# A list scheduler's stated durations and engine-to-engine times, both set to those of the trace: a two-block fp32 model on one core

## The chip, the cores and the metric

The kernel runs on one core of a Trainium2 chip. The metric is the device time of one execution in microseconds (us), taken as the median over runs. The core's engines are TensorE (PE, with its weight loads listed apart as PEld), VectorE (DVE), ScalarE (ACT), GpSimd (POOL) and SyncE (SP), which issues the large DMAs here. Each engine works through its own list of instructions in the order in which they were emitted; semaphores hold an instruction until what it reads is there.

## What is computed

Two blocks on 512 tokens of width 1024, all in fp32. Cut to its frame:

```python
def first_block(x, mem, ...):
    for i in range(2):
        h = _rms_norm(x, norm_mix_pre[i]); mem_n = _rms_norm(mem, mem_norm[i])
        if i == 0:
            mixed = _attention_sublayer(h, mem_n, ...)   # 12 heads of 64 in 3 dilated bands, relative bias
        else:
            mixed = _deltanet_sublayer(h, mem_n, ...)    # 6 heads of 128, both directions, chunked
        x = x + _rms_norm(mixed, norm_mix_post[i])
        h = _rms_norm(x, norm_ffn_pre[i])
        x = x + _rms_norm(_swiglu(h, ffn_w_gate_up[i], ffn_w_down[i]), norm_ffn_post[i])
    return x

def second_block(x, ...):
    h = rmsnorm(x, norm_g); proj = h @ w_in
    mix = concat([gla_mixer(...), s5_mixer(...), nsa_mixer(...)])
    return x + mix @ w_out
```

Both sublayers of the first block also attend to a memory of 256 rows and end in an output projection. In the DeltaNet sublayer a recurrent state runs over the chunks of a head:

```python
def step(state, inp):                       # one chunk
    v_new = uc - wc @ state
    out = (qc * exp(gc)) @ state + ac @ v_new
    state = state * exp(g_last) + (kc * exp(g_last - gc)).T @ v_new
```

## The kernel before

Activations live on chip as 128-partition tiles, transposed for the matmuls (`X`: 8 k-tiles of 128x512). Every large matmul is `mm3` (L265 to L273): each operand is a pair of high and low part in fp32r, and a product is three passes, L271 (high by low), L272 (low by high), L273 (high by high). The passes of 128x512 in such a triple are called rows below, three of them a triple. Weights come by SP's DMA into three `raw` buffers; ACT writes the high part (L243, `wh`), and DVE, or POOL for the pieces marked `aside`, the low part (L262, `wl`), each as two halves of 128x512; four pairs exist (`wsl`).

The layers follow one another in `layers` (from L1728): the attention front, `out_ffn` 0, the DeltaNet layer, `out_ffn` 1, the second block. `out_ffn` takes an output projection through `X` and the swiglu FFN behind it. `projector` (L1788 on) supplies projections that fill PE between the steps of the heads, with a large `late` (a low rank); the output projection of the layer belongs to the thread `trunk` and ranks lower still.

**What sets the order.** No order is written out by hand. Every piece of the program is a generator, a thread of the class `Flow` (L48 to L147). Before it emits an instruction it yields an engine, a stated cost, and the tokens that it waits for. A token holds a stated time and the engine that made it. `start` gives the earliest stated start: the time at which the engine is free, and for each token its time plus a stated way from engine to engine. `run` takes the operation with the earliest start, and among those of the same engine that could start within 0.1 of it the one with the lowest `late`. It books start plus cost as the end, on the engine and as the token of the thread, and lets the thread emit. So the stated numbers decide which instruction stands before which in each engine's list, and the chip then runs the lists as they are. The stated costs come from small formulas:

```python
def act(n, ap=0): return "ACT", 0.1 + n * 8.4e-4 + 0.1 * ap
def dve(n):       return "DVE", 0.07 + n * 1.05e-3
def pool(n):      return "POOL", 0.1 + n * 2.4e-3
```

and from numbers at the yields: 0.65 for a triple of 128x512 (0.33 for one of 256 columns), 0.22 for a single small matmul.

**Names that come up later.** At the start, x and the memory are normalized and transposed: `norm` makes the sum of squares on ACT, adds eps on DVE (L338, `iss`), raises to -1/2 on POOL (L340, `irs`), scales on DVE (L343, L346, `hs`), and PE transposes (L354, `hT`). The other norms do the same (L917 to L956; `hs` at L942, transpose L949, `Xh` and `Xl` L951, L956). In the front, L769 weights the heads' outputs and L796 makes the `Xl` that the output projection reads. In the DeltaNet layer `each` prepares a head: convolutions on DVE (four L1324 and one L1305 for each of key, query and value), decays (L1405, L1413, L1422) and the inverse of a unit triangular matrix by blocks (PE L1503, L1519, L1523, L1544, L1566; ACT L1530; DVE L1506, L1548, L1571). `chain` (L1594 to L1633) then walks four chunks for each direction d: PE L1594, DVE `rhs` L1597, PE L1602, ACT `vn` L1605, DVE `vs` L1610, PE L1612, DVE `St` L1616 or L1619, outputs at PE L1624 and L1625, summed at DVE L1629 (`otok`). `gate_out` (L1640 to L1661) normalizes a head's output (ACT L1651, POOL L1352 and L1658), transposes it (PE L1335, `poT`) and gates it; L1706 and L1708 split it into the `Xh`, `Xl` of the output projection. At the end of the second block, softmax units (L2720 to L2753) alternate with triples of the last output projection.

## Time and profile before

| | |
|---|---|
| median of 3 runs | 1763.38 us (1762.12 to 1763.65) |
| the profiled execution | 1761.48 us, span 1759.5 us, mean granted clock 0.993 |
| PE busy | 1708.7 us (97%) in 12031 matmuls |
| DVE, ACT, POOL busy | 979.8 us (56%), 763.2 us (43%), 338.0 us (19%) |
| chain that ended last | PE 84%, DVE 9%, ACT 2%, issue 2% |

A row of the timeline gives the start, the duration, engine and line, the operation and its tiles; xN stands for N alike in a row, with the time from the first start to the last end; the bracket is the engine's idle time before it and what ended that. A row of the waits gives for whom PE waited, the sum, the number of times and the longest. Windows give the busy time of each engine in a stretch, and PEclk, the share of the full clock that TensorE was granted.

### The profile page before, as it was taken

To read this page: it belongs to the slowest core of one execution; us is meant where nothing else is said; L and a number is where in the kernel's file an instruction comes from. 1 tells how busy PE (TensorE), PEld (TensorE's weight loads), DVE (VectorE), ACT (ScalarE), POOL (GpSimd) and SP (SyncE) were. 2 spreads that over 40 slices of the span, in tenths; PEclk is the share of its full clock that TensorE was granted. 3 is DMA by queue.
4 is the path that set the end of the run, shared out by engine and by line. 5 is a ranking of instruction groups with operands and counts; after the bars stand their busy time and mean duration, and the time that the engine had idled before them with its cause. 6 is when DMAs were issued, how large, how long until landed. Compare 5 with 4: busy or idle time off the path is not lost.

```text
span 1759.5 us, 30190 instructions
## 1 busy us (share of the span) xinstructions
PE 1708.7 (97%) x12031; PEld 1423.2 (81%) x12031; DVE 979.8 (56%) x1997; ACT 763.2 (43%) x1808; POOL 338.0 (19%) x496
## 2 busy tenths in 40 slices
PE   6999999999999999999999899999999999999999
PEld 5988679888888888788777788888888888888787
DVE  6333656323333378867887467464433468467573
ACT  5443635333223245656555355333223353345671
POOL 5200001000000021220222351364540033210000
PEclk9999999999999999999999999999999999999999
DMA  6513133333233332211110164345333253552012
GB/s 195 154 51 95 49 120 97 120 96 96 96 96 96 96 114 79 61 38 38 38 37 32 59 152 139 109 133 144 108 108 96 77 159 115 153 154 69 25 37 84
DMA packets 211981, 167.84 MB, mean 95 GB/s; under 512 B 21996, under 2 KB 183036, under 8 KB 211840
## 3 DMA queue, kind: packets, MB, share of 16 engines
q1 hardware_dynamic: 203808, 154.39, 29.7%
q0 software_dynamic: 4560, 9.42, 2.1%
q10 hardware_dynamic: 3472, 2.10, 0.4%
q8 instruction: 94, 1.54, 0.4%
q14 instruction: 47, 0.39, 0.1%
HBM read 152.23 MB, written 13.65 MB: 94 GB/s over the span
## 4 chain that ended last, share of the span: by engine, by line
PE 84%; DVE 9%; ACT 2%; issue 2%; DMA 1%; POOL 1%; ACTq 0%; SPq 0%; DVEq 0%; POOLq 0%
PE bk L271 23%; PE bk L272 22%; PE bk L273 22%; DVE hn L1324 2%; DVE wl L262 1%; PE no L2753 1%; PE npT L2736 1%; PE x L1519 1%; PE x L1523 1%; PE y L1544 1%; DVE hs L942 1%; PE ns L2722 1%; PE hT L949 1%; PE ns L2720 1%; PE o L1625 1%
## 5 line engine op out<-in xcount | busy, mean ns | idle before, releaser
L262 DVE TENSOR_TENSOR wl<-raw,wh 128x512 fp32r<-128x512 f32 x450 | 315.8, 742 | 372.4 <-ACT wh L243 371.8
L243 ACT ACTIVATE wh<-raw 128x512 fp32r<-128x512 f32 x474 | 273.0, 623 | 534.4 <-PE bk L273 300.4
L271 PE MATMUL bk<-Xh,wl 128*128 128x512 f32 (+2 forms) x1312 | 494.9, 377 | 0.2 <-ACT Xh L951 0.2
L272 PE MATMUL bk<-Xl,wh 128*128 128x512 f32 (+2 forms) x1312 | 478.4, 365 | 0.5 <-DVE Xl L956 0.5
L273 PE MATMUL bk<-Xh,wh 128*128 128x512 f32 (+2 forms) x1312 | 478.5, 365 | 0.0
L273 PEld LDWEIGHTS bk<-Xh,wh 128*128 128x128 f32 (+1 forms) x1312 | 246.9, 188 | 40.1
L271 PEld LDWEIGHTS bk<-Xh,wl 128*128 128x128 f32 (+1 forms) x1312 | 247.5, 189 | 39.0 <-issue 3.5
L272 PEld LDWEIGHTS bk<-Xl,wh 128*128 128x128 f32 (+1 forms) x1312 | 247.7, 189 | 34.8 <-DVE Xl L956 0.9
L271 PE MATMUL bk<-wh,Xl 128*128 128x512 f32 (+1 forms) x424 | 152.6, 360 | 6.7 <-DVE Xl L796 3.7
L272 PE MATMUL bk<-wl,Xh 128*128 128x512 f32 (+1 forms) x424 | 145.8, 344 | 0.3 <-DVE wl L262 0.2
L273 PE MATMUL bk<-wh,Xh 128*128 128x512 f32 (+1 forms) x424 | 145.2, 342 | 0.0
L271 PE MATMUL bk<-wh,Al 128*128 128x512 f32 x352 | 139.7, 397 | 0.0
L272 PE MATMUL bk<-wl,Ah 128*128 128x512 f32 x352 | 139.5, 396 | 0.0
L921 POOL TENSOR_TENSOR nc<-ncm,nhalf 128x1 f32<-128x1 f32 x16 | 11.5, 720 | 661.9 <-DVE ncm L919 661.9
L273 PE MATMUL bk<-wh,Ah 128*128 128x512 f32 x352 | 138.6, 394 | 0.0
L1093 DVE TENSOR_TENSOR sg<-sg,bk 128x512 f32<-128x512 f32 x44 | 30.2, 687 | 124.7 <-PE bk L273 120.2
L271 PEld LDWEIGHTS bk<-wh,Xl 128*128 128x128 f32 x424 | 84.7, 200 | 18.0 <-DVE Xl L796 3.1
L273 PEld LDWEIGHTS bk<-wh,Xh 128*128 128x128 f32 x424 | 84.8, 200 | 8.1
L272 PEld LDWEIGHTS bk<-wl,Xh 128*128 128x128 f32 x424 | 85.0, 200 | 7.6 <-DVE wl L262 1.0
L271 PEld LDWEIGHTS bk<-wh,Al 128*128 128x128 f32 x352 | 66.0, 188 | 16.1
L273 PEld LDWEIGHTS bk<-wh,Ah 128*128 128x128 f32 x352 | 66.0, 188 | 16.0
L272 PEld LDWEIGHTS bk<-wl,Ah 128*128 128x128 f32 x352 | 66.1, 188 | 15.4
(586 smaller groups left out, 2623.8 us busy)
## 6 DMA issues: line engine op xcount, KB each, us to landing
raw<-in_ffn_w_gate_up_dram SPq DMA_DIRECT2D x88, 512.0 KB, 3.9
raw<-in_ffn_w_down_dram SPq DMA_DIRECT2D x44, 512.0 KB, 3.3
raw<-in_dn_w_in_dram SPq DMA_DIRECT2D x27, 512.0 KB, 4.0
raw<-in_att_w_in_dram SPq DMA_DIRECT2D x20, 512.0 KB, 4.1
raw<-in_w_in_dram SPq DMA_DIRECT2D x20, 512.0 KB, 3.8
raw<-in_mem_w_kv_dram SPq DMA_DIRECT2D x8, 512.0 KB, 3.6
raw<-in_att_w_out_dram SPq DMA_DIRECT2D x8, 512.0 KB, 3.3
xd<-x SPq DMA_DIRECT2D x8, 512.0 KB, 2.6
```

The source lines that it names most:

```text
L243: nc.scalar.activation(wh[:, sl], ev["raw"][:, sl], AF.Copy)
L262: eng.tensor_tensor(wl[:, sl], raw[:, sl], wh[:, sl].bitcast(F32), op=OP.subtract)
L271: mm(out, A[1], B[0], start=first, stop=False, **kw)
L272: mm(out, A[0], B[1], start=False, stop=False, **kw)
L273: mm(out, A[0], B[0], start=False, stop=last, **kw)
L942: nc.vector.scalar_tensor_tensor(hh[:, hv[i]], x[:, t, hv[i]], r2, r["gain"][:, hv[i]], op0=OP.mult, op1=OP.mult)
L949: nc.tensor.transpose(p[:, k * P:(k + 1) * P], hh[:, i * 512 + k * P:i * 512 + (k + 1) * P], self.ident)
L1093: nc.vector.tensor_tensor(sg, sg, pu, op=OP.mult)
L1324: nc.vector.scalar_tensor_tensor(acc[:, d0:d1], raw[:, d0 + o:d1 + o], cw[:, ti, tap:tap + 1], acc[:, d0:d1], op0=OP.mult, op1=OP.add)
L1519: nc.tensor.matmul(dn8(b[i])[at], lhsT, rhs, start=True, stop=True)
L1523: nc.tensor.transpose(b[d][:, o:o + P], U[:, d, 2 * n:2 * n + 2, :].rearrange("p c q -> p (c q)"), self.ident)
L1544: nc.tensor.matmul(dn8(ys[par])[HB[f], d, n, :], T[d][HB[par], n, f, :], xs[f][HB[par], d, n, :], start=True, stop=True)
```

## The change

The ways from engine to engine are stated by pair: 0.2 from PE, 0.12 to PE, 0.04 between ACT, DVE and POOL (before: 0.2 for all), and nothing on the same engine (before: 0.07). Every DVE operation is booked 0.08 longer and every ACT operation 0.07 longer, on the engine too. A triple is booked at 0.682 and 0.36 in place of 0.65 and 0.33. Costs of POOL and of the DMA stay. No instruction is added, removed or changed; the engines' lists hold the same instructions in another order. With three lines more, L271 is L274 after the change, and so on.

```diff
-    HOP = 0.2
+    HOP = 0.04
+    FROM_PE, TO_PE = 0.2, 0.12
+    STEP = {"DVE": 0.08, "ACT": 0.07}
...
-            s = max(s, at + (self.HOP if e != eng else 0.0 if e == "PE" else 0.07))
+            s = max(s, at + (self.FROM_PE if e == "PE" else self.TO_PE if eng == "PE" else self.HOP) * (e != eng))
...
             eng, cost = t["req"][:2]
+            cost += self.STEP.get(eng, 0.0)
             self.free[eng] = s + cost
...
-                t = yield "PE", 0.65 * (t1 - t0) / S
+                t = yield "PE", 0.682 * (t1 - t0) / S
...
-                        t = yield "PE", 0.33
+                        t = yield "PE", 0.36
```

In the FFN stretches the lists stay as they were. Elsewhere matmul triples and steps of the heads change places. Three places follow.

POOL at the start: the powers (`irs`) of the token norms and the low parts of the first weights. Before:

```order
L340 TENSOR_TENSOR irs<-iss,nhalf 128x1
L262 TENSOR_TENSOR wl<-raw,wh 128x512 x3
L340 TENSOR_TENSOR irs<-iss,nhalf 128x1
L262 TENSOR_TENSOR wl<-raw,wh 128x512 x2
L340 TENSOR_TENSOR irs<-iss,nhalf 128x1
L262 TENSOR_TENSOR wl<-raw,wh 128x512 x2
```

After:

```order
L343 TENSOR_TENSOR irs<-iss,nhalf 128x1 x2
L265 TENSOR_TENSOR wl<-raw,wh 128x512 x3
L343 TENSOR_TENSOR irs<-iss,nhalf 128x1 x2
L265 TENSOR_TENSOR wl<-raw,wh 128x512 x2
L462 DMA bias_scr<-brow 4x3x384
```

The second of these powers stood behind three low parts and stands ahead of them now; PE's transposes of the token norms follow two by two.

DVE in the third head of the DeltaNet layer, where `chain` and the convolutions of a later head share it. Before:

```order
L1597 SCALAR_TENSOR_TENSOR rhs0_7948<-chain_7776,neg_5158,vtok_6811 128x128
L1324 SCALAR_TENSOR_TENSOR hn_7904<-craw_7902,convw_881,hn_7904 128x511
L1610 TENSOR_SCALAR vs1_7964<-vn1_7956,ksc_5156 128x128
L1324 SCALAR_TENSOR_TENSOR hn_7904<-craw_7902,convw_881,hn_7904 128x511
L1610 TENSOR_SCALAR vs0_7991<-vn0_7966,ksc_5156 128x128
L1616 SCALAR_TENSOR_TENSOR St1_7993<-St1_7884,etot_5157,chain_7820 128x128
```

After:

```order
L1600 SCALAR_TENSOR_TENSOR rhs0_7922<-chain_7745,neg_5160,vtok_6936 128x128
L1509 COPY_PREDICATED U_7746<-lm64_892,y0_7906 64x256 x2
L1308 SCALAR_TENSOR_TENSOR vTh_7609<-sqt_7904,hn_7630 128x512
L1613 TENSOR_SCALAR vs0_7961<-vn0_7935,ksc_5158 128x128
L1613 TENSOR_SCALAR vs1_7964<-vn1_7959,ksc_5158 128x128
L1327 SCALAR_TENSOR_TENSOR hn_7915<-craw_7913,convw_894,hn_7915 128x510
L1619 SCALAR_TENSOR_TENSOR St0_7976<-St0_7894,etot_5159,chain_7745 128x128
L1619 SCALAR_TENSOR_TENSOR St1_7979<-St1_7864,etot_5159,chain_7823 128x128
L1327 SCALAR_TENSOR_TENSOR hn_7915<-craw_7913,convw_894,hn_7915 128x511 x2
```

Both `vs` stood behind a convolution step each; now they stand together, behind other work of the inverse, and ahead of the convolution.

PE in the last head of the DeltaNet layer, where the chain of the head and the triples of the output projection (`wh`, `Xl`) meet. Before:

```order
L1612 MATMUL chain<-vs_9742,ktok 128x128
L1594 MATMUL chain<-St_9740,kTh 128x128
L1624 MATMUL o<-St_9710,qe_9081 128x128
L1625 MATMUL o<-vn_9735,AT_9055 128x128
L271 MATMUL bk<-wh,Xl 128x512
L272 MATMUL bk<-wl,Xh 128x512
L273 MATMUL bk<-wh,Xh 128x512
L1602 MATMUL chain<-rhs_9755,Uf 128x128
L1594 MATMUL chain<-St_9750,kTh 128x128
```

After:

```order
L1615 MATMUL chain<-vs_9764,ktok 128x128
L1627 MATMUL o<-St_9737,qe_9038 128x128
L1628 MATMUL o<-vn_9757,AT_9024 128x128
L1627 MATMUL o<-St_9742,qe_9172 128x128
L1628 MATMUL o<-vn_9761,AT_9133 128x128
L1597 MATMUL chain<-St_9767,kTh 128x128
L1597 MATMUL chain<-St_9772,kTh 128x128
L1605 MATMUL chain<-rhs_9781,Uf 128x128
L1605 MATMUL chain<-rhs_9783,Uf 128x128
```

The triples are gone from between the chain's steps: all 22 that stood from the head's L1544 to its `poT` now stand ahead of that L1544.

## Rows read from the trace of the kernel before

**Rows 1.** PE's waits: waiter, line, releaser; us in total, times, longest, whole span.

```profile
PE chain L1612 <- DVE vs L1610: 5.3, 5, 1.4
PE hT L949 <- DVE hs L942: 4.7, 9, 1.4
PE bk L271 <- DVE Xl L796: 3.7, 2, 2.8
...
PE hT L354 <- DVE hs L346: 2.8, 2, 2.3
```

**Rows 2.** Windows: startup, an FFN, the DeltaNet layer's two halves, the last softmax units.

```profile
core 0: us, PE busy (x) PEld busy (x) DVE busy (x) ACT busy (x) POOL busy (x), PEclk, DMA share, GB/s
0.00:48.00 48.00, 33.46 (x198) 29.00 (x199) 30.42 (x44) 27.91 (x52) 28.64 (x36) 0.93 0.67 198
...
290.00:630.00 340.00, 340.00 (x1536) 280.87 (x1536) 120.13 (x191) 103.37 (x188) 0.54 (x1) 1.00 0.33 99
...
684.00:860.00 176.00, 173.53 (x2004) 141.15 (x2004) 138.20 (x315) 107.15 (x293) 38.52 (x31) 0.99 0.17 46
860.00:979.00 119.00, 110.97 (x1521) 91.75 (x1519) 91.63 (x202) 63.21 (x175) 29.49 (x25) 0.97 0.12 37
```

**Rows 3.** Windows: two of the stretches at a lower clock, and the last softmax units.

```profile
31.60:38.40 6.80, 6.80 (x28) 5.36 (x27) 2.98 (x4) 1.94 (x5) 6.09 (x7) 0.50 0.56 190
...
943.00:946.40 3.40, 3.05 (x13) 2.84 (x14) 3.37 (x7) 0.28 (x1) 1.44 (x2) 0.50 0.00 0
...
1700.00:1718.00 18.00, 18.00 (x142) 14.30 (x142) 9.51 (x29) 11.37 (x46) 0.00 (x0) 1.00 0.01 1
```

**Rows 4.** Timeline of DVE at the start (start, us): two in a row, one.

```profile
12.03 1.28 DVE L367 TENSOR_TENSOR hn<-hT,gm 128x512 f32<-128x512 f32 x2
13.23 0.68 DVE L262 TENSOR_TENSOR wl<-raw,wh 128x512 fp32r<-128x512 f32 x1
```

**Rows 5.** Timeline of POOL at the start.

```profile
21.23 0.94 POOL L340 TENSOR_TENSOR irs<-iss,nhalf 128x1 f32<-128x1 f32 x1 [9.74 <-DVE iss L338]
22.16 5.24 POOL L262 TENSOR_TENSOR wl<-raw,wh 128x512 fp32r<-128x512 f32 x3
```

**Rows 6.** Timeline of all engines, third head of the DeltaNet layer.

```profile
859.20 1.44 DVE L1324 SCALAR_TENSOR_TENSOR hn<-craw,convw,hn 128x511 f32<-128x511 f32 x1
...
860.57 1.28 DVE L1610 TENSOR_SCALAR vs<-vn,ksc 128x128 f32<-128x128 f32 x1
...
861.90 0.38 PE L1612 MATMUL chain<-vs,ktok 128*128 128x128 f32 x1 [1.37 <-DVE vs L1610]
```

**Rows 7.** Timeline of PE, an earlier head: the chain's three links, with other work between.

```profile
747.49 0.61 PE L1594 MATMUL chain<-St,kTh 128*128 128x128 f32 x4
748.64 0.61 PE L1602 MATMUL chain<-rhs,Uf 128*128 128x128 f32 x4
749.78 0.42 PE L1612 MATMUL chain<-vs,ktok 128*128 128x128 f32 x2
...
751.70 0.39 PE L1612 MATMUL chain<-vs,ktok 128*128 128x128 f32 x2
752.62 0.38 PE L1594 MATMUL chain<-St,kTh 128*128 128x128 f32 x2
```

**Rows 8.** Timeline of PE, the last head of the DeltaNet layer.

```profile
976.61 0.33 PE L1544 MATMUL y<-xT 64*64 64x64 f32 x4 [0.94 <-ACT xT L1530]
...
978.43 0.47 PE L271 MATMUL bk<-wh,Xl 128*128 128x512 f32 x1 [0.66 <-DVE Xl L1708]
...
983.56 0.60 PE L1602 MATMUL chain<-vtok,Uf 128*128 128x128 f32 x4
...
997.50 0.39 PE L1602 MATMUL chain<-rhs,Uf 128*128 128x128 f32 x2
...
1006.28 0.50 PE L271 MATMUL bk<-wh,Xl 128*128 128x512 f32 x1 [2.23 <-DVE Xl L1708]
```

More of the change, by code (lines that the diff above doesn't have):

```diff
@@ L412, in memory @@
                         w, kk = W["mv"][l][k // 4]["W"], k % 4
-                        t = yield "PE", 0.33
+                        t = yield "PE", 0.36
                         self.mm3(p[:, :256], (M[l].h[:, k, ts], M[l].l[:, k, ts]), (w.h[:, kk, :], w.l[:, kk, :]),
@@ L623, in group @@
                     w, kk = W2[k // 4]["W"], k % 4
-                    t = yield "PE", 0.33
+                    t = yield "PE", 0.36
                     self.mm3(p[:, :256], (X.h[:, k, t0:t0 + P], X.l[:, k, t0:t0 + P]), (w.h[:, kk, :], w.l[:, kk, :]),
@@ L1118, in out_ffn @@
                             for k in range(KT):
-                                tk = yield "PE", 0.65 * (t1 - t0) / 512
+                                tk = yield "PE", 0.682 * (t1 - t0) / 512
                                 self.mm3(p[:, t0:t1], (ev["W"].h[:, k, :], ev["W"].l[:, k, :]),
@@ L1801, in part @@
             for k in range(KT):
-                t = yield "PE", 0.65 * (t1 - t0) / S
+                t = yield "PE", 0.682 * (t1 - t0) / S
                 self.mm3(it["p"][:m, t0:t1], (W.h[:, k, :], W.l[:, k, :]), (X.h[:, k, t0:t1], X.l[:, k, t0:t1]),
@@ L1839, in projector @@
                     W, kk = it[k // 4]["W"], k % 4
-                    t = yield "PE", 0.33
+                    t = yield "PE", 0.36
                     self.mm3(p[:, :256], (X.h[:, k, sl], X.l[:, k, sl]), (W.h[:, kk, :], W.l[:, kk, :]),
@@ L2398, in glu @@
                     for k in range(2):
-                        t = yield "PE", 0.65
+                        t = yield "PE", 0.682
                         self.mm3(p, (w.h[:, k, os_], w.l[:, k, os_]), yh[k], k == 0, k == 1)
```

## The prediction

> **What bounds the kernel now.** I read the page first: PE is busy for 97% of the span, so a new order can win no more than PE's idle time and its slow-clock time, while it can lose as much as it uncovers. The windows say where the idle time lies. An FFN stretch has none (340 us busy of 340), and the lists are unchanged there, so I cost it at nothing. The startup has 48 - 33.46 = 14.5 us, of which the first wait for data is outside the change. The DeltaNet layer has 2.5 us in its first half and 119 - 110.97 = 8.0 us in the second [rows 2]. The list of waits then says on what: the chain's L1612 behind DVE's `vs` (5.3 us), the norm transposes L949 (4.7), the output projection behind L796 (3.7), the start's transposes L354 behind the wider scalings (2.8) [rows 1]. Last, the windows at a lower clock: for 6.8 us at the start and in pieces of 3.4 us later, the granted clock is 0.50, half of 2.4 GHz, each time just behind a cluster of such waits [rows 3]. A piece of 3.4 us at half rate does 1.7 us of work, so it loses 1.7 us.
>
> **What the change does to each term.** No instruction is added, so PE's work is the same sum; I only count idle time. The sum is made against the profiled execution, 1761.48 us; the median of the runs is 1.9 us above it, and I add that at the end.
>
> First, are the new numbers truer? In a pair, two DVE operations of 128x512 take 1.28 us together, but one alone 0.68 [rows 4]: a second one begins 0.60 after the first. The old formula gives 0.07 + 512 x 0.00105 = 0.608 for one, the spacing. The new one books 0.688, the whole duration, as time in which DVE can take nothing else. As latency that is right; as occupation it is 0.08 too much for every operation that follows another directly. The path PE to DVE to PE keeps its stated length (0.2 + c + 0.2 before, 0.2 + c + 0.08 + 0.12 after). So the scheduler now believes that DVE is fuller than the rows show. Where many small DVE steps share the engine, which is the DeltaNet layer (138 us busy of 176, then 92 of 119 [rows 2]), it expects the heads later and gives PE's early slots to projections. That is what the lists show: projections move ahead and the heads' steps back.
>
> *Startup.* POOL's second power of the token norms waited behind three low parts, 5.24 us of POOL [rows 5]; it now stands ahead of them. At best this takes the wait of the transposes behind L346, 2.8 us [rows 1], and part of the 3.4 us that the slow clock costs behind it [rows 3]. Against it, the memory's matmuls, which filled PE between the transposes, are now bunched ahead of them, and POOL's low parts come later. From -4 to +3; I take -1.
>
> *End of the attention front.* The low parts of two weights move ahead of the last head's statistics on DVE. The wait behind L796 is 3.7 us [rows 1]: -2.8 if its longest goes, +3 if it doubles; I take +1, since what moved ahead of the statistics lies on their path.
>
> *Norm chains.* The transposes L949 move up, with three to six rows less of matmuls in front of them, while `hs` stands ahead of other DVE work. Their wait is 4.7 us in 9 places [rows 1]; -2 to +2, and I take +0.5.
>
> *DeltaNet.* This is the main term and has two sides. The tail: in the profile, from the last head's L1544 to the first triple that needs that head takes 1006.28 - 976.61 = 29.7 us [rows 8], and 22 triples of the output projection are spread through it. A triple costs 340 / 1536 x 3 = 0.66 us [rows 2], so 14.6 us of this are cover. After the change all 22 stand ahead of L1544 and the chain runs bare. What does it take then? L1544 to the first L1602 took 7.0 us with five triples in it; between 3.7 without them and 7.0, I take 5.2. Each of three further chunks has the links L1594 to L1602 (1.15), L1602 to L1612 (1.14) and L1612 to L1594 (0.92) [rows 7], 9.6 in all. From the last L1602 to the next triple took 8.8 us [rows 8], most of it the output's norm and transpose, which no triple shortens. Sum 23.6. The 14.6 us of triples run ahead of it, so the layer ends 23.6 + 14.6 - 29.7 = 8.5 us later, unless they fill idle time there.
>
> The other side is what they can fill. The two windows hold 2.5 + 8.0 us of idle, less the 0.94 and 0.66 at L1544 and the triple behind it, which belong to the tail [rows 2, 8]: 8.9 us; and two pieces at half clock (864 and 943 us) lost 1.7 each, 3.4. All 12.3 gone would leave 8.5 - 12.3 = -3.8. One wait shows how it can go: L1612 waited 1.37 us because `vs` had a convolution step of 1.44 ahead of it on DVE and itself took 1.28, three to five times its usual length, beside POOL's work [rows 6]; the new list has both `vs` ahead of the convolution. But the heads' steps themselves move back by 6 to 16 us of PE work, so some waits move along. I take half of the 8.9 us, 4.5, and none of the clock: 8.5 - 4.5 = +4. The bad end takes nothing off and adds one more slow piece behind the bare chain, 8.5 + 1.7 = +10.2.
>
> *Last softmax units.* Eight triples leave the stretch 1700 to 1718 us for the end. PE was busy for all 18 us, ACT for 11.4 [rows 3]. Without 8 x 0.66 = 5.3 us PE has 12.7 us of work there, hardly more than ACT has, and its units wait for ACT's exponentials. From 0 to +4; I take +2. The triples run at the end at their own length, which is no loss.
>
> Sum: -1 + 1 + 0.5 + 4 + 2 = +6.5, so 1768.0 for such an execution and 1769.9 beside the median; I say 1770.
>
> **A rule against the row.** The spacing above rests on pairs that start 0.60 apart and last 0.68 each [rows 4]. The Trainium skill, "VectorE: DVE Perf Modes", section "The DRAIN you can't avoid", says that the next operation does not start until the pipe is empty. By that rule the new booking would be the true occupation, the heads would really come as late as the new order has them, and the triples pulled ahead would fill real gaps; this case's pairs speak against it, and it is weighed as part of the first rival.
>
> **The rivals.**
> *Faster.* DVE limits the heads more than its share says (`vs` at 1.28 us is a sign [rows 6]), so the triples pulled ahead fill all 8.9 us of waits and both slow pieces: DeltaNet -3.8; the earlier power gives -3 at the start; the rest is nil. 1763.4 - 6.8 = 1756.6. For it: the waits that the new list removes are real. Against it: the tail is bare in the list, and this needs every gap filled. By the rule above this is what comes, 1757. Chance 0.27.
> *No change.* Fillers only trade places: the 14.6 us of triples pay for the tail of 8.5 by 8.5 of the 12.3, and start, front and softmax cancel. 1763, from 1760 to 1767. Chance 0.23.
> *My forecast,* slower, 1767 to 1776. Chance 0.32.
> *Much slower.* The pulled-ahead triples stand where PE had no gap, and the heads' chains arrive late again and again: DeltaNet +10.2, start +2, front +2, softmax +3, norms +1, thus 1763.4 + 18.2 = 1781.6. It decides at the point where the triples absorb less than 4.5 us. Chance 0.18.
>
> That the change does not do what it says, in that a stated number has no effect, is excluded: the lists differ.
>
> **How the numbers follow.** The likeliest case is slower; its own range is 1767 to 1776. A measurement of this kernel can tell about 0.2%, 3.5 us, from no change. Faster by more is the first rival, 0.27; within it the second, 0.23; slower 0.32 + 0.18 = 0.50. The ends: all good bounds together would give -4 - 2.8 - 2 - 3.8 = -12.6, all bad ones +3 + 3 + 2 + 10.2 + 4 = +22. Leaving a tenth on either side I take 1754 to 1782.
>
> **What would show it.** In the profile of the changed kernel: (1) between the last head's L1547 (L1544 before) and the first triple behind its `poT`, no row of 128x512 and 22 to 25 us in place of 29.7, with 12 to 14 us of PE idle; if it is 18 or less, the bare links are shorter than I read them. (2) In the DeltaNet layer ahead of that, idle of 4 to 5 us in place of 8.9; near zero means the first rival, 9 or more the last. (3) At the start, PE waits less behind the wider `hs`, and the slow-clock stretch is shorter than 6.8 us. (4) In the last softmax units PE waits for ACT for 1 to 3 us. (5) FFN stretches as before to within 0.5 us; were they longer, the cause would lie outside this reasoning. (6) DVE pairs still start 0.60 apart. The prediction is wrong if the fillers absorb more than 9 us, or if some stretch that the lists leave alone changes.

## The result, and the profile after

The changed kernel takes 1781.36 us (median; 1778.93 to 1783.96), the kernel before, timed beside it, 1762.75 us. The ratio is 1.0112 with a 95% interval of 1.0088 to 1.0135: 18.6 us slower. The forecast was 6.6 us slower. The sign was right, the time lies just inside the range of 1754 to 1782, and the size is wrong by a factor of almost three. The profiled execution of after lasted 1783.96 us, the longest of its runs, so it shows 22.5 us against the 1761.48 us of before; the sums below are made between these two and are some 4 us larger than the medians tell.

The page of after, first its engines and the slices of PE:

```profile
PE 1718.9 (96%) x12031; PEld 1430.5 (80%) x12031; DVE 978.5 (55%) x1997; ACT 759.9 (43%) x1804; POOL 340.9 (19%) x496
...
PE   6999989999999999999999799999999999999999
```

PE has the same 12031 matmuls; one slice in the middle shows 7. To see where the time comes in, the start times of the same matmuls in both traces serve as landmarks. First the groups of before (line, engine, tiles, count: ns min/median/max, first and last start in us):

```profile
L271 PE MATMUL bk<-wh,Al x352: 392/394/484, 345.7 to 1415.0; 128*128 128x512 f32 x176
L1602 PE MATMUL chain<-vtok,Uf x24: 270/275/348, 742.1 to 983.9; 128*128 128x128 f32 x24
L1335 PE MATMUL poT<-ident,otok x24: 271/273/328, 769.9 to 1003.8; 128*128 128x128 f32 x24
L2108 PE MATMUL gs<-gq,gk x64: 217/217/266, 1451.1 to 1453.4; 32*64 32x64 f32 x64
L2736 PE MATMUL npT<-ident,nP x160: 270/273/331, 1618.5 to 1714.1; 128*128 128x128 f32 x160
```

And of after, where the lines are three higher:

```profile
L274 PE MATMUL bk<-wh,Al x352: 393/394/484, 349.3 to 1429.7; 128*128 128x512 f32 x176
L1605 PE MATMUL chain<-vtok,Uf x24: 270/275/554, 744.5 to 996.1; 128*128 128x128 f32 x24
L1338 PE MATMUL poT<-ident,otok x24: 270/272/421, 772.3 to 1015.6; 128*128 128x128 f32 x24
L2111 PE MATMUL gs<-gq,gk x64: 217/217/266, 1467.3 to 1470.1; 32*64 32x64 f32 x64
L2739 PE MATMUL npT<-ident,nP x160: 270/273/331, 1636.5 to 1732.5; 128*128 128x128 f32 x160
```

The first group is the down projections of the two FFNs, the second and third the first and last head of the DeltaNet layer, the fourth the start of the second block's mixers, the fifth its softmax. The differences, stage by stage:

| stage | forecast, us | measured, us |
|---|---|---|
| start to the first down projection of FFN 0 (349.3 - 345.7) | 0 (-1 and +1) | +3.6 |
| to the first chain step of DeltaNet (2.4 - 3.6) | 0 | -1.2 |
| to the last `poT` of DeltaNet (11.8 - 2.4) | +4 | +9.4 |
| to the last down projection of FFN 1 (14.7 - 11.8) | +0.5 | +2.9 |
| to the first `npT` of the softmax (18.0 - 14.7) | 0 | +3.3 |
| to the end of the span (22.7 - 18.0) | +2 | +4.7 |
| sum | +6.5 | +22.7 |

(The norm chains' +0.5 belongs to several stages and stands in one.) The windows of after that answer to those of before [rows 2, 3]: startup, FFN 0, the DeltaNet layer up to the last head's L1547, the slow stretch in that head, the last softmax units. Columns as in [rows 2]:

```profile
0.00:48.00 48.00, 33.26 (x196) 27.88 (x197) 29.74 (x45) 28.60 (x52) 29.42 (x36) 1.00 0.67 200
293.50:633.50 340.00, 340.00 (x1536) 280.80 (x1535) 119.28 (x189) 103.03 (x187) 0.54 (x1) 1.00 0.33 100
687.40:866.00 178.60, 175.95 (x2009) 143.25 (x2007) 140.67 (x315) 106.50 (x292) 42.79 (x33) 0.98 0.17 45
866.00:991.00 125.00, 120.59 (x1576) 99.71 (x1574) 88.22 (x205) 66.65 (x179) 26.34 (x23) 0.99 0.11 35
994.50:1004.70 10.20, 9.24 (x36) 8.08 (x36) 4.20 (x15) 2.22 (x8) 0.00 (x0) 0.50 0.01 2
1718.00:1733.70 15.70, 14.34 (x136) 11.15 (x135) 10.56 (x33) 12.19 (x52) 0.00 (x0) 1.00 0.01 2
```

The clock of the startup is now 1.00 in place of 0.93, the FFN is full as before, and a stretch of 10.2 us at half clock lies in the last head. PE's waits over the whole span, which answer to [rows 1]:

```profile
PE hT L952 <- DVE hs L945: 8.6, 7, 2.7
PE chain L1615 <- DVE vs L1613: 5.6, 6, 2.5
...
PE poT L1338 <- POOL otok L1661: 4.4, 1, 4.4
PE fbc L767 <- DVE amx L759: 3.0, 1, 3.0
PE bk L274 <- DVE Xl L1711: 2.2, 1, 2.2
...
PE bk L274 <- DVE Xl L799: 1.6, 1, 1.6
```

The transposes behind `hs` wait 8.6 us in place of 4.7, the chain as much as before, the last head's `poT` 4.4 us for POOL, where triples stood in front of it before. Last, PE in the last head of after, the place of [rows 8]:

```profile
990.49 0.27 PE L1547 MATMUL y<-xT 64*64 64x64 f32 x2
...
994.81 0.77 PE L1605 MATMUL chain<-vtok,Uf 128*128 128x128 f32 x2 [0.46 <-DVE Uf L1574]
...
999.72 1.22 PE L1605 MATMUL chain<-rhs,Uf 128*128 128x128 f32 x4
...
1005.06 0.85 PE L1605 MATMUL chain<-rhs,Uf 128*128 128x128 f32 x4
...
1008.71 0.75 PE L1605 MATMUL chain<-rhs,Uf 128*128 128x128 f32 x4 [0.22 <-DVE rhs L1600]
1014.93 1.06 PE L1338 MATMUL poT<-ident,otok 128*128 128x128 f32 x4 [4.36 <-POOL otok L1661]
1018.22 0.80 PE L274 MATMUL bk<-wh,Xl 128*128 128x512 f32 x1 [2.23 <-DVE Xl L1711]
```

No triple stands between the first and the last of these rows, as the list said. The bare run takes 1018.22 - 990.49 = 27.7 us, where 22 to 25 were forecast; before, it took 29.7 with triples in it, 21 of them by its trace and not 22. Each chunk of the chain, from L1605 to L1605, takes 4.9, 5.3 and 3.65 us; the first two lie in the half-clock stretch, the third behind it.

### The profile page after: what moved, and what is told of

It reads as the page before. It is cut to its first block, busy times and chain, and to the rows that moved or that the text cites. A ratio compares the mean times of both kernels' runs of the same rounds, so it can differ in the third digit from the quotient of the medians.

```text
span 1782.2 us, 30187 instructions
## 1 busy us (share of the span) xinstructions
PE 1718.9 (96%) x12031; PEld 1430.5 (80%) x12031; DVE 978.5 (55%) x1997; ACT 759.9 (43%) x1804; POOL 340.9 (19%) x496
## 4 chain that ended last, share of the span: by engine, by line
PE 86%; DVE 7%; ACT 2%; issue 2%; POOL 1%; DMA 1%; ACTq 0%; DVEq 0%; POOLq 0%
PE bk L274 23%; PE bk L275 22%; PE bk L276 22%; DVE wl L265 1%; PE x L1522 1%; PE x L1526 1%; PE no L2756 1%; PE npT L2739 1%; PE y L1547 1%; DVE hs L945 1%; PE o L1628 1%; PE chain L1605 1%; DVE x L928 1%; PE chain L1615 1%; PE ns L2725 1%
## 5 line engine op out<-in xcount | busy, mean ns | idle before, releaser
L265 DVE TENSOR_TENSOR wl<-raw,wh 128x512 fp32r<-128x512 f32 x450 | 321.9, 755 | 376.7 <-ACT wh L246 375.9
L274 PE MATMUL bk<-Xh,wl 128*128 128x512 f32 (+2 forms) x1312 | 495.1, 377 | 0.2 <-DVE wl L265 0.2
L274 PEld LDWEIGHTS bk<-Xh,wl 128*128 128x128 f32 (+1 forms) x1312 | 247.8, 189 | 39.0 <-issue 3.8
L274 PE MATMUL bk<-wh,Xl 128*128 128x512 f32 (+1 forms) x424 | 152.9, 361 | 5.5 <-DVE Xl L1711 2.2
L924 POOL TENSOR_TENSOR nc<-ncm,nhalf 128x1 f32<-128x1 f32 x16 | 10.3, 643 | 678.2 <-DVE ncm L922 675.8
L274 PE MATMUL bk<-wh,Al 128*128 128x512 f32 x352 | 139.8, 397 | 0.0
L274 PEld LDWEIGHTS bk<-wh,Xl 128*128 128x128 f32 x424 | 84.4, 199 | 18.2 <-issue 3.1
L274 PEld LDWEIGHTS bk<-wh,Al 128*128 128x128 f32 x352 | 66.1, 188 | 16.0
```

Of the source, the lines that this page charges most:

```text
L265: eng.tensor_tensor(wl[:, sl], raw[:, sl], wh[:, sl].bitcast(F32), op=OP.subtract)
L274: mm(out, A[1], B[0], start=first, stop=False, **kw)
```

## Experiments

Three questions: in which stages does the loss arise, which of the stated numbers makes it, and by what mechanism does the DeltaNet layer lose. The expectations name their theories by letters and say what each holds. Ten of the eighteen times lie outside every range that was set for them. Eight of these are above: the step alone, the step as latency, the way left at 0.2, 0.19, the window of 0.35, the triples held back, more triples (by 0.2 us) and the dummies. Two lie between the ranges: the passes left out and the halved window. "Before" and "after" with a time are always medians; a place in the trace is compared between profiled executions.

### Stage by stage

Each of these runs gives the scheduler the new numbers in one stage and the old ones elsewhere, through a switch that the program sets as it passes from stage to stage:

```diff
+    def numbers(self, new):
+        Flow.NEW = new
...
-            s = max(s, at + (self.HOP if e != eng else 0.0 if e == "PE" else 0.07))
+            way = ((0.2 if e == "PE" else 0.12 if eng == "PE" else 0.04) * (e != eng) if self.NEW else
+                   0.2 if e != eng else 0.0 if e == "PE" else 0.07)
+            s = max(s, at + way)
...
+            cost += {"DVE": 0.08, "ACT": 0.07}.get(eng, 0.0) * self.NEW
...
-                        t = yield "PE", 0.33
+                        t = yield "PE", (0.36 if Flow.NEW else 0.33)
```

**New numbers in the DeltaNet layer alone** (on at its start, off behind the last head):

```diff
+                F.numbers(not F.NEW)
                 eK, eP, close = self.deltanet(F, W1, order1, eX, res)
...
+            if h == 5:
+                F.numbers(not F.NEW)
```

> The kernel before, with the new stated numbers used only while the DeltaNet layer is put in order (from the trunk's entry into it to the end of its last head) and the old ones everywhere else. Theory A (the DeltaNet layer loses by itself, because the last head's chain stands bare in PE's list): 8.5 us slower than before, 1771, the stretch from the last head's last block of the inverse to the first triple behind its poT bare and near 27 us, part of it at half clock. Rival B (the loss is spread: any new order loses some at every place, and the layer's share only shows up together with the rest): 1763 to 1766.

1770.24 us against 1763.03, ratio 1.0047 [1.0032, 1.0062]. In its trace the first chain step comes 1.0 us earlier than in before, the last `poT` 6.5 us later, and the last down projection of FFN 1 9.4 us later; nothing is given back after that. So the layer and the norms behind it lose 7 to 9 us by themselves.

**Old numbers in the DeltaNet layer alone,** the same switch set the other way round:

> The changed kernel, with the old stated numbers used only while the DeltaNet layer is put in order. Theory A: 8.5 us less than the changed kernel, about 1773, with 21 triples back between the last head's steps; what is left (+10 or so over before) lies in the norm chains and in the second block. Rival B: within 3 us of the changed kernel, 1778 to 1784.

1773.08 us, ratio 1.0061 [1.0046, 1.0076]. That was the expected 1773. It puts 10.1 us of the loss, about half of the 18.6, outside the DeltaNet layer, where the forecast had +2.5 in all.

**New numbers up to the DeltaNet layer:**

> The kernel before with the new stated numbers up to the DeltaNet layer and the old ones from there on. Theory A: 2 to 5 us slower than before, 1765 to 1768, and the parts by stage (this one, the DeltaNet layer alone with 7 and the second block alone) add up to the whole change, 16 to 20. Rival: the later stages lose as well, 1770 or more.

1766.83 us, ratio 1.002 [1.0009, 1.0032]. The trace is 3.7 us late at the first down projection and 3.7 us late at the end: a loss of the front is carried to the end unchanged.

**New numbers in the second block:**

> The kernel before with the new stated numbers from the second block on, the old ones ahead of it. Theory A (each stage loses by its own order): 6 to 9 us slower than before, 1769 to 1772, of which 3 to 5 us from the last softmax units to the end. Rival (the second block only inherits its loss): within 3 us of before.

1770.07 us against 1763.06, ratio 1.0035 [1.0015, 1.0055]. Of the 8.5 us between the profiled spans, 3.6 have come by the first `npT` and 4.9 come behind it. This stretch of its trace lies ahead of the softmax (columns as in [rows 2]):

```profile
1480.00:1500.00 20.00, 18.73 (x282) 14.52 (x281) 13.99 (x32) 6.79 (x16) 8.00 (x6) 0.83 0.16 44
```

Full clock would give 1.00, as before has it there; a mean of 0.83 over 20 us is 6.8 us at half clock. PE's idle time from 1440 us to the first `npT` grew from 1.6 to 3.3 us, so 1.7 of the 3.6 us are waits, and the other 1.9 lie in matmuls that take longer at the lower clock.

The three parts multiply to 1.0020 x 1.0047 x 1.0035 = 1.0102, within the interval of the whole. So the loss is made stage by stage, in each by itself.

### Number by number

**The added step alone** (0.08 on DVE, 0.07 on ACT), ways and matmuls as before:

```diff
+    STEP = {"DVE": 0.08, "ACT": 0.07}
...
+            cost += self.STEP.get(eng, 0.0)
```

> Only one third of the change: each DVE operation booked 0.08 and each ACT operation 0.07 longer, on the engine too; the ways between engines and the cost of a triple as before. Theory A (the booked time on DVE and ACT makes the scheduler expect the heads late): the tail of the DeltaNet layer is bare here too, at least 8 us slower than before, 1771 to 1780. Rival C (the short ways of 0.04 are what loses): within 3 us of before, 1760 to 1766.

1798.36 us, ratio 1.0198 [1.0181, 1.0215]: nearly twice the loss of the whole change.

**The matmuls' stated length alone** (0.682 and 0.36 for 0.65 and 0.33):

```diff
-                t = yield "PE", 0.65 * (t1 - t0) / S
+                t = yield "PE", 0.682 * (t1 - t0) / S
```

> Only the third part of the change: a triple booked at 0.682 and 0.36 in place of 0.65 and 0.33, with the old ways and no lengthening of DVE and ACT. These are the spacings that the trace shows. Theory S: 5 to 25 us slower than before, though the number is truer. Rival T: as before or faster, 1755 to 1765.

1783.41 us, ratio 1.0119 [1.0089, 1.0148]: as much as the whole change, by another part.

**The change with the way between engines other than PE left at 0.2:**

```diff
-    HOP = 0.04
+    HOP = 0.2
```

> The changed kernel with the way between ACT, DVE and POOL set back from 0.04 to 0.2; all else as changed. Its last head keeps four triples and none in the chain. If the norm chains (DVE to POOL to DVE to ACT) lose because 0.04 makes the scheduler place their transposes too early: the waits of L952 behind hs go from 8.6 back to 5 us and the kernel gains 3 to 6 us, 1775 to 1778. If the order is lost by any new number, the norm chains' waits are of any size and the time is 1775 to 1795.

1798.0 us, ratio 1.0202 [1.0182, 1.0223]. So the parts do not add: the step alone and the matmuls alone lose more together than the whole, and taking one part back makes the whole worse. A cause that is bound to one number would not do this. As far as these runs show, what the lists have in common is that they are other lists. The ways between engines were not changed alone.

**Small changes of one number of before.** If any other list loses, a number that means next to nothing must cost time too. The way from engine to engine, 0.2, in before:

```diff
-    HOP = 0.2
+    HOP = 0.19
```

> The kernel before with one number changed by a twentieth: 0.19 in place of 0.2 for every way from engine to engine. In its list of PE the last head's chain is bare too. Theory A (what costs is where the triples land, and not whether the numbers are true): the DeltaNet layer loses 6 to 9 us by this alone and the kernel is 1768 to 1775. Rival C (the loss comes from the size of the change in the numbers): 1762 to 1765.

1787.44 us, ratio 1.0142 [1.0122, 1.0163]. Here too the chain of the last head is bare: no triple stands between its first step and its `poT`. But this time the chain keeps full clock (columns as in [rows 2], then the first and the last L1602 on PE):

```profile
993.90:1004.67 10.77, 8.22 (x56) 6.92 (x56) 6.36 (x23) 2.62 (x10) 0.00 (x0) 1.00 0.01 2
993.90 0.46 PE L1602 MATMUL chain<-vtok,Uf 128*128 128x128 f32 x2 [0.46 <-DVE Uf L1571]
...
1004.67 0.75 PE L1602 MATMUL chain<-rhs,Uf 128*128 128x128 f32 x4 [0.22 <-DVE rhs L1597]
```

The same steps take 10.8 us, against 13.9 in after. From the first chain step of the layer to its last `poT` this run takes 263.3 us, 1.6 more than before and not the expected 6 to 9: a bare last head does not by itself cost the layer its 9.4 us. The larger losses of this run lie elsewhere, 5.9 us by the first chain step and 16.3 behind the last `poT`. Then 0.201:

```diff
-    HOP = 0.2
+    HOP = 0.201
```

> The kernel before with one number changed by half a per cent: 0.201 in place of 0.2 for every way from engine to engine. Theory S (the lists are so sensitive to the stated numbers that any change of them gives another draw, and the draw of before is a good one): 5 to 25 us slower, 1768 to 1788, with losses in the DeltaNet layer and in the second block. Rival T (the time depends on how true the numbers are): the same as before, within 2 us.

1775.34 us, ratio 1.0066 [1.0041, 1.009]: half a per cent of one stated number costs 11.6 us. In its trace 1.0 us have come by FFN 0, 6.8 by the first chain step, 4.2 by the last `poT`, 7.7 by the softmax, 14.1 by the end: a gain in the DeltaNet layer, losses in the other stages. And 0.21:

```diff
-    HOP = 0.2
+    HOP = 0.21
```

> The kernel before with 0.21 in place of 0.2 for every way. Its PE list keeps 39 triples under the last head, as before (38). Theory C: the DeltaNet layer ends within 3 us of before, and what is lost lies elsewhere; in all 1765 to 1780 by theory S. Rival: the layer loses 6 us or more although it has its cover.

1775.26 us, ratio 1.0075 [1.0046, 1.0104]. Between the landmarks of the DeltaNet layer this run takes 261.6 us, as long as before (261.7), and loses elsewhere. The loss does not grow with the distance from 0.2: it is 24.8 us at 0.19, 11.6 at 0.201 and 13.2 at 0.21.

**The rule's own margin.** Half the window in which the scheduler prefers the lower `late`, in before:

```diff
-DELTA = 0.1
+DELTA = 0.05
```

> The kernel before with its own numbers, and the margin within which the lower `late` wins set to 0.05 in place of 0.1. 22 triples stand under the last head. Theory C: the layer ends 6 to 11 us later than before. Theory S: the other stages lose too, in all 1773 to 1790. Rival T (true or old numbers make the order, not the margin): within 3 us of before.

1768.55 us (1763.98 to 1773.93, a wide scatter), ratio 1.0029 [1.0015, 1.0043]. And three and a half times the window, in after, in case the new numbers only want a wider one:

```diff
-DELTA = 0.1
+DELTA = 0.35
```

> The changed kernel with its new numbers, but an operation of a lower `late` may be taken if it can start within 0.35 of the earliest, in place of 0.1, so that PE's slot may go to a head's step that is about to be ready. 35 triples stand under the last head. Theory G (the greedy rule lets triples overtake the heads, and true numbers only show it): the DeltaNet layer loses no more than 2 us against before, and the kernel is 1763 to 1775. Theory S (any new order is another draw): the layer may gain, but other stages lose, 1775 to 1795.

1826.43 us, ratio 1.0369 [1.0352, 1.0386]; 20 us of it had come by the first down projection.

With after these are ten lists that come from before by other numbers over the whole program, and all ten are slower, by 6 to 64 us.

### What the DeltaNet layer loses by

**Less PE work in it.** If PE's work set the layer's length, leaving work out would shorten it by that much; if the heads' own steps did, not at all. In before, the middle one of the three passes is left out for every second k-tile of the layer's projections. That is 124 matmuls, 92 of 512 columns and 32 of 256, worth 108 of 128x512 or about 24 us:

```diff
+        if not thin:
+            mm(out, A[0], B[1], start=False, stop=False, **kw)
...
-                         k == 0, k == KT - 1)
+                         k == 0, k == KT - 1, thin=not haste and k % 2)
```

> The kernel before, in its own order, with one of the three passes left out for every second k-tile of the DeltaNet layer's projections: 108 matmuls of 128x512 less, 24 us of PE's work in this layer (the low part of the weights' product is incomplete there). Theory D: the path of the inverses stays, PE idles for what was left out, and the time falls by no more than 10 us, 1753 to 1763. Rival P: it falls by 20 to 24 us, 1739 to 1743.

1748.99 us against 1763.79, ratio 0.9923 [0.9893, 0.9954]: by the medians 14.8 of 24 us come back. Between the profiled executions it is 10.3, and all of it has come by the last `poT` (10.7). So the layer is neither: about half of what PE is spared shows. Much of the rest turns into waits, as PE's idle time over the span grows from 50.8 to 59.5 us.

**More ACT work in the heads.** In before, the second copy of every pair of the inverse (L1530) is made twice, which adds 36 ACT operations of up to 128x512:

```diff
-                    nc.scalar.activation(z[i][:, lo:], b[i][:, lo:], AF.Copy)
+                    for _ in range(1 + i):
+                        nc.scalar.activation(z[i][:, lo:], b[i][:, lo:], AF.Copy)
```

> The kernel before, in its own order, with one ACT copy made twice in each of the six steps of each head's inverse (the second one writes the same values again): 36 copies of some 0.53 us, 19 us if they lie on the path, on an engine that is busy 43% of the time. Theory D (the six inverses, one behind the other, are the path that sets the DeltaNet layer's length, and PE's triples only fill it): 12 to 19 us slower, 1775 to 1782, all of it between the first inverse and the last poT. Rival P (the layer is as long as PE's work, and ACT has room): 0 to 4 us slower.

1765.99 us against 1763.79, ratio 1.0013 [1.0001, 1.0025]. One such group in its timeline (start, us):

```profile
757.33 1.71 ACT L1531 ACTIVATE xT<-x 128x512 f32<-128x512 f32 x3 [0.94 <-PE x L1523]
```

Three copies take 1.71 us, so 36 more are some 19 us of ACT, of which 2.2 show. Over the first five heads the first chain steps come 0.3 to 1.3 us later than in before; the last chain's come 3.5 us later (987.4 against 983.9), and 3.3 us later the span ends. So the path of the inverse is covered nearly everywhere but in the last head: the theory that it paces the layer falls, and what the last head loses is lost.

**The step as latency, not as occupation.** The forecast held that booking 0.08 as time in which DVE takes nothing else is what makes the heads late. In after, the step is added to the token's time alone:

```diff
-            cost += self.STEP.get(eng, 0.0)
             self.free[eng] = s + cost
-            t["tok"] = (s + cost, eng)
+            t["tok"] = (s + cost + self.STEP.get(eng, 0.0), eng)
```

> The changed kernel, but the 0.08 and 0.07 lengthen only the stated time at which the result is there, and the engine is booked for the old cost. Theory A: the triples are back in the last head's chain, DeltaNet loses nothing, and if the norm chains and the second block lose by the same booking, 1760 to 1766; if they lose by the ways of 0.04, 1770 to 1776. Rival C: 1775 to 1784, as the ways are unchanged.

1793.22 us, ratio 1.0168 [1.0146, 1.019]. The stretch from the first chain step to the last `poT` takes 265.7 us in place of 271.1 in after (261.7 in before), so there the booking accounts for up to 5 us; but the second block and the softmax behind it lose far more than that gains, and the kernel is slower than after. As an account of the whole loss the booking falls.

**Triples held back for the last head.** In after, the output projection may begin only when the last head's last inverse step has been emitted:

```diff
+                if l == 5 and h == 5:
+                    self.eH["tok"] = ty
...
-                yield "wait", eP, eK[6]
+                yield "wait", eP, eK[6], self.eH
```

> The changed kernel with its new numbers everywhere, but the output projection of the DeltaNet layer may not begin before the last head has reached the last step of its inverse, so that 21 triples stand between this head's steps again. Theory A (the bare tail is the DeltaNet layer's whole loss): the triples cover the tail, which costs 12.6 us less, and no longer fill the 4 us of earlier waits that they filled: about 8 us less than the changed kernel, 1773, and the end of the stage at the time of the kernel before plus 3. Rival (the heads are late anyway, and the triples only wait for them in another place): 1779 to 1783.

1785.2 us against 1762.68, ratio 1.0129 [1.0114, 1.0144]: no gain on after. Windows of after, then of this run, ahead of the last chain and in it (columns as in [rows 2]):

```profile
956.00:986.00 30.00, 29.92 (x387) 25.33 (x391) 15.88 (x43) 11.64 (x32) 2.05 (x2) 0.94 0.06 19
986.00:1019.00 33.00, 23.65 (x216) 18.90 (x207) 11.27 (x34) 7.18 (x25) 8.29 (x11) 0.78 0.06 17
```

```profile
956.00:986.00 30.00, 24.63 (x412) 20.47 (x414) 16.66 (x44) 12.62 (x34) 2.46 (x2) 0.86 0.07 20
986.00:1019.00 33.00, 27.82 (x187) 22.59 (x179) 10.27 (x32) 6.11 (x23) 7.53 (x10) 0.86 0.05 17
```

Idle time in the chain falls from 9.35 to 5.2 us, and in the 30 us ahead it rises from 0.1 to 5.4: those triples had covered the inverse. The same triples cannot stand in both places.

**More triples for it.** The only other store is the layer's projections: the last two z projections, 16 triples, wait until the last inverse starts, again in after:

```diff
+            if not haste and i == len(items) - 2:
+                yield "wait", self.eI
```

> The changed kernel, but the last two projections of the DeltaNet layer (the gates z of two heads, 16 triples) may not begin before the last head's inverse does. Under the last head, from its inverse to its poT, there are then 33 triples in PE's list in place of 21 (before: 38). Theory C (what is lost is PE work under the last head, 0.68 us a triple): up to 8 us less than the changed kernel, 1773 to 1777. Theory L (the heads come late by their own steps; triples held back only bring the idle time forward): the last inverse starts no earlier than at 955 us and the time is 1779 to 1784.

1784.23 us against 1762.1, ratio 1.013 [1.0114, 1.0146]. The last `poT` comes 2.0 us earlier than in after, the last down projection of FFN 1 only 0.8, the end 0.2. Cover moved by hand gains little, and that little is given back.

**The clock kept up.** Behind every chain matmul of the last head in after stand two dummy matmuls of 128x128 into an unused part of the bank:

```diff
+            def warm(n):
+                for _ in range(n * (h == 5)):
+                    nc.tensor.matmul(b[:, 3 * P:], kT[:, 0:P], kt[:, 0, :], start=True, stop=True)
...
+                    warm(2)
```

> The changed kernel with added work that nobody reads: behind each matmul of the last head's chain two matmuls of 128x128 into an unused quarter of the same bank, so that PE has work in the bare tail and keeps its clock. Theory A (of the 27.7 us of the tail, some 4 come from the half clock granted there): the granted clock stays full for more of the tail, the tail takes 23 to 25 us, and the kernel gains 2 to 5 us, 1776 to 1779. Rival (the links wait on DVE, ACT and POOL, and PE's clock is beside the point; the added work stands in the way): the tail takes 28 us or more and the time is 1781 to 1786.

1787.0 us against 1762.68, ratio 1.0138 [1.0122, 1.0155]. Windows of its last head and the last two chunks on PE:

```profile
995.00:998.40 3.40, 3.37 (x16) 3.40 (x17) 1.20 (x5) 0.55 (x2) 0.00 (x0) 0.51 0.02 5
998.40:1018.50 20.10, 15.67 (x134) 15.10 (x133) 6.88 (x23) 3.94 (x18) 2.04 (x3) 1.00 0.08 27
```

```profile
1001.18 0.43 PE L1610 MATMUL chain<-rhs,Uf 128*128 128x128 f32 x2
...
1006.47 0.43 PE L1610 MATMUL chain<-rhs,Uf 128*128 128x128 f32 x2
...
1011.76 0.43 PE L1610 MATMUL chain<-rhs,Uf 128*128 128x128 f32 x2
```

The clock is back after 3.4 us, but a chunk takes 5.3 us at full clock with the dummies between its steps, the same as after's 5.3 at half clock without them, and after's third chunk, at full clock and bare, 3.65. So the clock does cost the bare chain something, 4.9 + 5.3 - 2 x 3.65 = 2.9 us; the run with 0.19, bare and at full clock throughout, gives 13.9 - 10.8 = 3.1. The dummies cost as much or more.

## Why the prediction was right in sign and wrong in size

**Right.** (1) The last head runs bare, though for longer than was said, and PE idles for 9.4 us of it, where 12 to 14 were forecast. (3) The startup's slow stretch is gone: the window of after has clock 1.00 where [rows 3] show 0.50. (4) In part: in the last softmax units PE idles, 1718.0 to 1733.7 us has 14.3 us of PE in 15.7, against 18.0 in 18.0 [rows 3]; of these 1.4 us, waits for ACT are 0.7 and one for DVE 0.4. (5) FFN 0 is 340 us of 340. (6) DVE pairs are as before [rows 4]; two at another place of after:

```profile
1060.63 1.28 DVE L959 TENSOR_TENSOR Xl<-hT,Xh 128x512 fp32r<-128x512 f32 x2
```

A second one still begins 0.60 after the first, which lasts 0.68. So the rule that was weighed against it, in the Trainium skill's "VectorE: DVE Perf Modes", "The DRAIN you can't avoid", does not describe these pairs; the section itself adds that a next operation that is not held starts earlier, and the trace agrees with that. The first rival, faster, which leaned on the rule, did not come.

**Wrong: the length of the bare tail.** The forecast had 23.6 us; it is 27.7. By its own three parts: L1547 to the first chain step 4.3 (5.2 taken), the four chunks up to the last L1605 13.9 (9.6), from there to the triple 9.5 (8.8). The step that failed is the chunk's price. The links of [rows 7] came from a head with its clock at full and summed to 3.2 us; the one chunk of after at full clock takes 3.65 and the two at half clock 4.9 and 5.3. So 2.9 of the 4.3 us are the half clock, and 1.4 are links read too short. The forecast put the clock behind the chain, as its bad end of +1.7, and not into it. The run with 0.19 bears this out: there the same bare chain keeps full clock and takes 10.8 us, and its stretch from L1544 to the triple behind `poT` takes 24.8, three triples in it, inside the 22 to 25 that were forecast. Before, the same 13.9 us as in after pass between those landmarks (997.50 - 983.56 in [rows 8]) with triples between the links: they held the chain up no more than the half clock does, so their going shortened nothing. The forecast had both numbers in its rows and took 4.3 us off for it. What decides whether a bare chain keeps its clock these runs do not show.

**Wrong, in smaller part: what the moved triples fill.** 4.5 us were taken. The trace of before has 21 triples in the tail and not 22; where four follow each other there, they start 0.69 apart, so 21 are 14.5 us, and the term of 14.6 hardly moves. The layer lost 9.4, and 27.7 + 14.5 - 29.7 = 12.5, so the triples pulled ahead absorbed 3.1. By idle time it is less: 2.65 + 4.4 = 7.1 us ahead of the tail, where 4 to 5 were forecast and before had 8.9, so 1.8 absorbed. `vs` before L1612, here in the fifth head, is one example: the list has it ahead of the convolution, as [rows 6] would want it, and in after it meets two halves of a weight instead:

```profile
953.77 2.04 DVE L265 TENSOR_TENSOR wl<-raw,wh 128x512 fp32r<-128x512 f32 x2 [1.00 <-ACT wh L246]
955.73 0.47 DVE L1613 TENSOR_SCALAR vs<-vn,ksc 128x128 f32<-128x128 f32 x2
956.06 0.71 PE L1615 MATMUL chain<-vs,ktok 128*128 128x128 f32 x4 [2.54 <-DVE vs L1613]
```

One wait is taken away and another, longer one comes: the chain's waits are 5.6 us in place of 5.3. The forecast had this as the way of its last rival, and that rival, 1781.6, is nearest to what came; but it put 10.2 of its 18.2 us into the DeltaNet layer, and the layer has 9.4 of 22.7.

**Wrong, in the larger part: the stages taken as nothing or nearly nothing.** Outside the DeltaNet layer 2.5 us were forecast and 13.3 came (in the profiled executions; by medians 10.1, from the run with the old numbers in the layer). Where it lies:
- Up to FFN 0, +3.6 for 0. The slow stretch at the start went, but the start won nothing by it; at 140 us the two traces stand level. The front's end lost: its transposes `fbc` wait 3.0 us for `amx` where nothing of the kind was among the long waits of before, and there are two slow pieces of 3.4 us in place of one.
- From the last `poT` to the end of FFN 1, +2.9 for +0.5. The waits behind `hs` there are 2.2 us in place of 0.5, one of 1.5 behind `wh` is new, and 6.8 us at half clock stand where 3.4 stood.
- Ahead of the softmax, +3.3 for 0. The forecast did not cost this stage at all. In after PE's listed waits there are 4.2 us in place of 1.5, and a slow piece of 3.4 us is new; the run on the second block alone shows the same two causes.
- Behind the first `npT`, +4.7 for +2. The softmax takes as long as before, 96.0 us against 95.6 from the first to the last `npT`, although seven of the moved triples, 4.8 us, left this stretch; one or two other triples and sixteen small matmuls, 1.1 us, came in. Behind the last `npT` stand 64 triples in place of 57, and that part takes 49.7 us in place of 45.4. So what was moved out came on top almost whole. That ACT sets the pace of the softmax, as the forecast took it, is not shown: PE's listed waits behind the first `npT` grow only from 0.3 to 1.6 us, 1.2 of them for ACT. The forecast's +2 came from splitting the difference between 0 and +4; 12.7 us of PE against 11.4 of ACT in [rows 3] could have been read as "hardly any room".

**The step behind these.** All of them are one mistake in method. The forecast costed only the differences between the lists that it could name, and let the others count as zero with equal chances both ways. The runs show that this is false for this kernel: a stated way of 0.201 for 0.200, which says nothing new about the chip, costs 11.6 us; ten lists drawn with other numbers all lose; and by stages, most of the small moves lose, though not all: with 0.201 the DeltaNet layer gains 2.6 us. The two smallest changes, 0.201 and the halved window, cost 11.6 and 6.4 us, so a list drawn anew was to be taken as that much slower before any term was counted. That truer numbers make a better list, the idea behind the change, was tested in parts: the step alone, the matmuls alone and the change without its short ways all lost. The ways alone were not run.

**Open.** Why the list of before is better than all its neighbours that ran is not settled by these runs. A margin that is wider or narrower, a step booked in another way, and numbers nearer to the trace or farther from it all lost; it fits with numbers that were picked by the time they gave, but no run here shows that.

## What to carry to other kernels

Where a greedy scheduler draws static lists for engines at 97%, its stated numbers can act, as here, less like a model to be made truer than like a seed: measure first what a meaningless change of half a per cent does, and take that, with its sign, as the price of any new list. To cost a chain that loses its cover, take its links at the clock that a bare chain gets, and compare with the time that it took under cover; here the bare chain was no shorter at half clock, and 3.1 us shorter where it kept full clock. When work leaves a stretch, ask whether the stretch will get shorter; where it does not, as in the softmax here, the work costs its full time wherever it goes.

## What the runs showed of the hardware

- A bare chain can lose its clock: in after it had 10.2 us at half clock, granted 0.50, while PE was 9.24 of 10.2 us busy by the records, where the slow pieces of before last 6.8 us at the start and 3.4 later. It need not: with 0.19 the same bare chain was granted 1.00 and took 10.8 us in place of 13.9. With small dummy matmuls the half clock lasted 3.4 us, and a chunk took 5.3 us all the same, as against 3.65 bare at full clock.
- 19 us of additional ACT work in the heads cost 2.2 us in all.
- Two weight halves on DVE took 2.04 us in the fifth head of after, against 1.28 for two operations of this size elsewhere [rows 4]; the runs do not show why.
